# Up projections of four feed-forward blocks from seven products of quarters in place of eight, with the down projections in three groups

## The chip, the cores and the metric

The kernel runs on one NeuronCore of a Trainium2 chip. The metric is the time of one execution on the device in microseconds, taken as the median of several runs. TensorE (PE) multiplies, VectorE (DVE), ScalarE (ACT) and GpSimd (POOL) work elementwise, and SyncE (SP) issues nearly all transfers.

## The reference

Two layers of a hybrid model on 512 tokens of width 1024, all in float32. Each layer has a feed-forward block (FFN), a mixer (attention of several kinds) and a second FFN; a norm follows at the end. The change touches only the four FFNs.

```python
def swiglu_ffn(x, g, w_gate, w_up, w_down):      # w_gate, w_up: 1024 x 2816; w_down: 2816 x 1024
    h = rmsnorm(x, g)
    return (jax.nn.silu(h @ w_gate) * (h @ w_up)) @ w_down

for i in range(DEPTH):
    x = x + 0.5 * swiglu_ffn(x, ffn1_norm[i], ...)
    x = x + mixer(rmsnorm(x, mix_norm[i]), ...)   # even_mixer for i = 0, odd_mixer for i = 1
    x = x + 0.5 * swiglu_ffn(x, ffn2_norm[i], ...)
return rmsnorm(x, final_norm)
```

## The kernel before

The activations stand transposed: x is eight tiles of 128 features by 512 tokens. To keep float32 accuracy, every operand is split into a high part and the rest (low part), and each product is three matmuls (mm3, lines 309 to 312): high by high, high by low, low by high. A weight tile takes a transfer (raw), a cast on ACT for the high part (wh, L305) and a subtraction on DVE for the low part (wl, L306). The norm is folded in: x times its gain is split into xg, and the reciprocal root mean square of each token (rb, a row that is broadcast to all partitions and copied from PSUM by ACT, L546) is multiplied onto the results.

An FFN is a loop over eleven pairs of hidden tiles (256 of the 2816 columns each). For a pair, gate_up_pair makes the gate product into two PSUM tiles psS and the up product into two tiles psT: 96 matmuls of 512 columns. Behind them, for each half, stands a chain over three engines: DVE multiplies gate by rb (L603), ACT takes silu (L604), POOL multiplies by rb again (L605), DVE multiplies by up (L607), ACT casts the result (L484), and DVE subtracts for its low part (L485). After six pairs, and after the other five, the down projection runs over the hidden tiles made so far (proj_T, results transposed, 512 columns wide). In the last FFN the down is proj_N, whose results are in natural order and which uses matmuls of 256 columns.

The mixers' weights are split ahead of time during the FFNs (cut_ahead): a generator whose units are taken between pairs and between downs, each of which loads a weight tile into buffers of its own (craw, ch, cl), splits it and stores both parts to memory.

A program of instructions for each engine is built ahead of time by a scheduler, which chooses an order for each engine from the code and the dependencies. On the chip every engine then runs its instructions strictly in that order, each waiting for the semaphores of what it needs. A tile has a tag with a fixed number of buffers (W_BUFS = 3 for wh and for wl), and a tile that reuses a buffer waits for its last reader.

Of the kernel before, what the change touches and what calls it, by code (L numbers as in the profile page):

```python
# [64 lines left out]
def hybrid_kernel(tc, x_in, positions, ffn1_norm, ffn1_w_gate, ffn1_w_up, ffn1_w_down, mix_norm,  # L65
# [4 lines left out]
    with ExitStack() as ctx:  # L70
# [6 lines left out]
        def nm(p):  # L77
            cnt[0] += 1
            return f"{p}_{cnt[0]}"
# [469 lines left out]
        def update(c, ps, scale, nxt):  # L549
            if scale == 1.0:  # L550
                nc.vector.tensor_add(x[c], ps, x[c])  # L551
            else:
                nc.vector.scalar_tensor_tensor(x[c], ps, scale, x[c], op0=ALU.mult, op1=ALU.add)
            if nxt is not None:
                nxt.add(c)


        def gate_up_pair(wg, wu, f0, norm, first):
# [49 lines left out]
                ats.append(split(a))  # L608
            return ats

        def ffn(norm, wg, wu, wd, nxt, hook=None, ahead=iter(()), per=1):

            f0 = 0
            for npair in (6, 5):
                at = []
                for k in range(npair):
                    at += gate_up_pair(wg, wu, f0 + 256 * k, norm, f0 == 0 and k == 0)
                    if hook is not None and f0 == 0:
                        next(hook, None)
                    if f0 or k > 1:  # L620
                        run(take(ahead, per))
                for d0 in range(0, D, 256):
                    run(proj_T(wd[f0:f0 + 256 * npair], at, d0,
                               lambda c, ps: update(c, ps, 0.5, nxt if npair == 5 else None)))
                    if npair == 6 or d0 < 512:
                        run(take(ahead, per))
                f0 += 256 * npair

        def final_ffn(norm, wg, wu, wd):
            gf = [tile_("pt", F32), tile_("pt", F32)]  # L630
            for hf in range(2):
                nc.scalar.dma_start(gf[hf], final_norm[hf * 512:(hf + 1) * 512].unsqueeze(0).to_broadcast([P, 512]))
            xn = [[tile_("m", F32), tile_("m", F32)] for _ in range(NT)]
            f0 = 0
            ssq, part, rn = small(4 * NT), small(NT), small(NT)

            def natural(t):
# [38 lines left out]
                    nc.sync.dma_start(out[t * P:(t + 1) * P, 512:1024], xn[t][1])  # L676
                return f

            for npair in (6, 5):
                at = []  # L680
                for k in range(npair):
                    at += gate_up_pair(wg, wu, f0 + 256 * k, norm, f0 == 0 and k == 0)
                    if f0 == 0 and 1 <= k <= 4:
                        natural(k - 1)
# [3 lines left out]
                f0 += 256 * npair  # L688


        def quarter_tiles():
# [721 lines left out]
```

## Time and profile before

| | |
|---|---|
| median of 3 runs | 2021.73 us (2020.76 to 2022.83) |
| the profiled execution | 2025.57 us |
| its span, first to last instruction | 2023.8 us |
| PE busy | 1983.0 us, 98% of the span |
| DVE busy | 1049.1 us, 52% |
| ACT busy | 771.3 us, 38% |
| POOL busy | 343.7 us, 17% |
| mean granted TensorE clock | 0.995 of 2.4 GHz |

The stages follow each other: the first FFN takes about 43 to 395 us, the even mixer to 684, the second FFN about 694 to 1064, the third 1075 to 1415, the odd mixer 1424 to 1640, the last FFN 1645 to 2018. The share of an engine over the whole span says little where stages differ, so the rows below are taken by stage. Matmuls are pipelined: the profile's duration of one (.39 us for 512 columns) is longer than the distance between the starts of two, and it is the distance that counts. L numbers are lines of the kernel that is profiled; in the changed kernel the same statements stand one line lower up to line 608 (L604 there is L603 here) and further down behind the new functions.

### The profile page before, as it was taken

How to read it: one execution, taken by the hardware profiler on the slowest of the kernel's cores; microseconds unless marked ns; L12 is line 12 of the kernel's file. 1: busy time of each engine (PE TensorE's matmuls, PEld its weight loads, DVE VectorE, ACT ScalarE, POOL GpSimd, SP SyncE). 2: the span in 40 equal slices, each digit the busy share in tenths (PEclk: the TensorE clock that was granted, in tenths of full speed). 3: DMA queues.
4: the chain of work that ended last, by engine and by line, in shares of the span. 5: the costliest groups of instructions: out<-in, count | busy, mean ns of one | idle time of the engine just before them, and what ended most of it. 6: DMA issues, size and time to landing. Idle time of an engine off the chain costs nothing.

```text
span 2023.8 us, 27480 instructions
## 1 busy us (share of the span) xinstructions
PE 1983.0 (98%) x10555; PEld 1708.0 (84%) x10555; DVE 1049.1 (52%) x1871; ACT 771.3 (38%) x1358; POOL 343.7 (17%) x412
## 2 busy tenths in 40 slices
PE   8999999999899999999999999999999999999998
PEld 6888888998888788888888888888999888899888
DVE  6654556446697634334353432344798754332433
ACT  5443344225577423213242231232346744221323
POOL 3110011223234211001121100111222321100112
PEclk9999999999999999999999999999999999999999
DMA  8998998792201423323323232223522243322321
GB/s 275 330 292 290 361 356 310 251 319 80 84 32 53 150 81 96 101 94 95 99 89 115 91 107 94 85 87 95 207 85 105 94 133 88 102 85 93 98 85 48
DMA packets 223604, 290.18 MB, mean 143 GB/s; under 512 B 25880, under 2 KB 191472, under 8 KB 223472
## 3 DMA queue, kind: packets, MB, share of 16 engines
q1 hardware_dynamic: 216544, 282.01, 42.0%
q10 hardware_dynamic: 6736, 6.37, 1.0%
q8 instruction: 83, 1.36, 0.3%
q14 instruction: 49, 0.40, 0.1%
q0 software_dynamic: 192, 0.04, 0.0%
HBM read 230.11 MB, written 58.26 MB: 142 GB/s over the span
## 4 chain that ended last, share of the span: by engine, by line
PE 87%; DVE 6%; DMA 2%; ACT 2%; issue 2%; POOL 1%; SPq 0%; ACTq 0%; POOLq 0%; DVEq 0%
PE psB L310 11%; PE psB L312 11%; PE psB L311 11%; PE psS L310 8%; PE psS L311 8%; PE psS L312 8%; PE psT L310 8%; PE psT L311 8%; PE psT L312 8%; PE psC L782 2%; PE psT L772 1%; DVE f L1241 1%; PE psS L747 1%; PE psS L746 1%; DVE sm L1240 1%
## 5 line engine op out<-in xcount | busy, mean ns | idle before, releaser
L306 DVE TENSOR_TENSOR wl<-raw,wh 128x1024 fp32r<-128x1024 f32 (+1 forms) x276 | 338.2, 1246 | 100.2 <-ACT wh L305 96.0
L305 ACT ACTIVATE wh<-raw 128x1024 fp32r<-128x1024 f32 (+1 forms) x276 | 274.8, 1013 | 206.2 <-PE psB L311 110.4
L605 POOL TENSOR_TENSOR p<-p,p 128x512 f32<-128x512 f32 x88 | 117.7, 1337 | 1026.0 <-ACT p L604 1026.0
L310 PE MATMUL psS<-xg,wh 128*128 128x512 f32 x704 | 275.9, 393 | 2.9 <-DVE x L551 2.1
L312 PE MATMUL psS<-xg,wl 128*128 128x512 f32 x704 | 274.4, 391 | 2.4 <-DVE wl L306 2.4
L311 PE MATMUL psS<-xg,wh 128*128 128x512 f32 x704 | 274.8, 391 | 0.9 <-DVE xg L507 0.9
L310 PE MATMUL psT<-xg,wh 128*128 128x512 f32 x704 | 274.5, 390 | 0.0
L312 PE MATMUL psT<-xg,wl 128*128 128x512 f32 x704 | 274.3, 390 | 0.0
L311 PE MATMUL psT<-xg,wh 128*128 128x512 f32 x704 | 274.2, 390 | 0.0
L310 PE MATMUL psB<-f,wh 128*128 128x512 f32 x528 | 205.4, 389 | 0.0
L311 PE MATMUL psB<-f,wh 128*128 128x512 f32 x528 | 205.4, 389 | 0.0
L312 PE MATMUL psB<-f,wl 128*128 128x512 f32 x528 | 205.4, 389 | 0.0
L603 DVE TENSOR_TENSOR p<-psS,p 128x512 f32<-128x512 f32 x88 | 60.3, 685 | 279.4 <-PE psS L312 270.2
L604 ACT ACTIVATE p<-p 128x512 f32<-128x512 f32 x88 | 55.6, 632 | 360.5 <-DVE p L603 359.8
L312 PEld LDWEIGHTS psS<-xg,wl 128*128 128x128 f32 x704 | 132.3, 188 | 31.2 <-DVE wl L306 3.7
L310 PEld LDWEIGHTS psS<-xg,wh 128*128 128x128 f32 x704 | 132.4, 189 | 30.6 <-DVE x L551 2.6
L311 PEld LDWEIGHTS psS<-xg,wh 128*128 128x128 f32 x704 | 132.5, 188 | 28.7 <-DVE xg L507 2.1
L311 PEld LDWEIGHTS psT<-xg,wh 128*128 128x128 f32 x704 | 132.5, 188 | 27.7
L312 PEld LDWEIGHTS psT<-xg,wl 128*128 128x128 f32 x704 | 132.4, 188 | 27.6
L310 PEld LDWEIGHTS psT<-xg,wh 128*128 128x128 f32 x704 | 132.3, 188 | 27.6
L310 PE MATMUL psB<-wh,xg 128*128 128x256 f32 x512 | 149.0, 291 | 0.4 <-PE psB L312 0.4
L312 PE MATMUL psB<-wh,xg 128*128 128x256 f32 x512 | 146.9, 287 | 0.0
(259 smaller groups left out, 3596.1 us busy)
## 6 DMA issues: line engine op xcount, KB each, us to landing
raw<-in_ffn_w_gate_dram SPq DMA_DIRECT2D x80, 512.0 KB, 5.1
raw<-in_ffn_w_up_dram SPq DMA_DIRECT2D x80, 512.0 KB, 5.0
raw<-in_ffn_w_down_dram SPq DMA_DIRECT2D x136, 256.0 KB, 3.7
cuth<-ch SPq DMA_DIRECT2D x44, 512.0 KB, 5.8
cutl<-cl SPq DMA_DIRECT2D x44, 512.0 KB, 5.8
wl<-cutl SPq DMA_DIRECT2D x44, 512.0 KB, 3.7
wh<-cuth SPq DMA_DIRECT2D x44, 512.0 KB, 4.4
raw<-in_ffn_w_down_dram SPq DMA_DIRECT2D x20, 512.0 KB, 3.5
```

The source lines that it names most:

```text
L305: pin(nc.scalar.activation(h[:, :n], raw[:, :n], AF.Copy))
L306: pin(nc.vector.tensor_sub(l[:, :n], raw[:, :n], h[:, :n].bitcast(F32)))
L310: nc.tensor.matmul(ps, lh, rh, start=start, stop=False)
L311: nc.tensor.matmul(ps, lh, rl, start=False, stop=False)
L312: nc.tensor.matmul(ps, ll, rh, start=False, stop=stop)
L603: nc.vector.tensor_mul(g, psg[f], rb)
L604: nc.scalar.activation(g, g, AF.Silu)
L605: nc.gpsimd.tensor_mul(g, g, rb)
L746: nc.tensor.matmul(bank[i], q[:, tsl], kh[:, 0:w], start=True, stop=False)
L747: nc.tensor.matmul(bank[i], q[:, tsl], kl[:, 0:w], start=False, stop=True)
L772: nc.tensor.transpose(ps[:, o:o + P], pr[i][:, j * P:(j + 1) * P], ident)
L782: nc.tensor.matmul(job["accs"][0][:, j * P:512], v(j), hl[j][part], start=first, stop=last)
```

## The change

Pair 0 of each FFN stays as it is, and behind it the sums of x are made once (class Sums, L627 to L637 of the changed kernel): from four pairs of x tiles, tokens 0 to 255 and 256 to 511, the right-hand terms of Strassen's products. For pairs 1 to 10 the up product (a 256 x 1024 by 1024 x 512 product) comes from seven products of quarters (seven): four sums of weight quarters on DVE (L681 to L684), their high and low parts (L665 on ACT, L666 on DVE), seven times 12 matmuls of 256 columns, and the combination of the results out of PSUM by two copies on ACT (L698, L702) and seven DVE operations. The seven results share four PSUM tiles psS: products 1 and 2, 3 and 5, 6 and 7 in one each. The gate product is as before, now in psT, behind the seven in the code. The activations of these pairs are L735 to L741. The down projection runs in three groups of 4, 4 and 3 pairs; in the last FFN the first two of them use proj_T. W_BUFS and RAW_BUFS are 4, the tag p has 8 buffers, and the cuts of the mixers' weights use the weights' buffers and are taken at pairs 4, 5, 8 and 9 and between downs.

```diff
+GROUPS = ((0, 4), (4, 8), (8, 11))
-SB_BUFS = {'xg': 18, 'f': 36, 'm': 8, 'p': 9, 'pt': 9}
+SB_BUFS = {'xg': 18, 'f': 36, 'm': 8, 'p': 8, 'pt': 9}
-W_BUFS = 3
-RAW_BUFS = 3
+W_BUFS = 4
+RAW_BUFS = 4
...
-                _, h, l = load_cut(src, a, b, rows, ("craw", "ch", "cl"), 2, 2)
+                _, h, l = load_cut(src, a, b, rows, ("raw", "wh", "wl"), RAW_BUFS, W_BUFS)
...
+        class Sums:
...
+            def make(self):
+                a, b = slice(0, 256), slice(256, 512)
+                for c in range(4):
+                    y = [tile_("p", F32) for _ in range(2)]
+                    for i in range(2):
+                        nc.scalar.activation(y[i], x[c + 4 * i], AF.Copy,
+                                             scale=gcol(self.norm.which, self.norm.layer, c + 4 * i))
+                    t = sb.tile([P, 1024], F32, tag="s7", bufs=3, name=nm("t7"))
+                    u1, u2, u3, u4 = (t[:, i * 256:(i + 1) * 256] for i in range(4))
+                    nc.vector.tensor_sub(u1, y[0][:, a], y[0][:, b])
+                    nc.vector.scalar_tensor_tensor(u2, u1, -1.0, y[1][:, b], op0=ALU.mult, op1=ALU.subtract)
+                    nc.vector.tensor_sub(u3, y[1][:, b], y[0][:, b])
+                    nc.vector.scalar_tensor_tensor(u4, u2, -1.0, y[1][:, a], op0=ALU.mult, op1=ALU.subtract)
+                    h, l = (sb.tile([P, 1024], F32R, tag="t7" + k, bufs=4, name=nm("t7" + k)) for k in "hl")
+                    nc.scalar.activation(h, t, AF.Copy)
+                    nc.vector.tensor_sub(l, t, h.bitcast(F32))
...
+        def seven(w, f0, sums, z):
...
+            parts(quarter(h1, 0), quarter(l1, 0), a11)
...
+            parts(h2, l2, raw[1])
...
+            nc.vector.tensor_add(s1, a21, a22)
+            nc.vector.tensor_add(s2, s1, a11)
+            nc.vector.tensor_add(s4, s2, a12)
+            nc.vector.tensor_add(s3, a11, a21)
+            for t, ns in ((u, (3, 5)), (v, (6, 7))):
+                h, l = new("wh", F32R, W_BUFS), new("wl", F32R, W_BUFS)
+                parts(h, l, t)
...
+            bank = [ps_tile("S") for _ in range(4)]
+            q = {n: bank[i // 2][:, (i % 2) * 256:(i % 2) * 256 + 256] for i, n in enumerate((1, 2, 3, 5, 6, 7, 4))}
...
+            for n in (1, 2, 3, 5, 6, 7, 4):
+                for c in range(4):
+                    mm3(q[n], st[n][0][:, c], st[n][1][:, c], *sums.term[n][c], c == 0, c == 3)
+                if n == 1:
+                    nc.scalar.copy(k1, q[1])
+                elif n == 2:
+                    nc.vector.tensor_add(z[0][:, a], q[2], k1)
+                elif n == 3:
+                    nc.scalar.copy(k3, q[3])
+                elif n == 5:
+                    nc.vector.tensor_add(k3, q[5], k3)
+                elif n == 6:
+                    nc.vector.tensor_add(k6, q[6], k1)
+                    nc.vector.tensor_add(z[0][:, b], k6, k3)
+                elif n == 7:
+                    nc.vector.tensor_add(k6, q[7], k6)
+                    nc.vector.tensor_add(z[1][:, b], q[5], k6)
+                else:
+                    nc.vector.tensor_add(z[1][:, a], q[4], k6)
+
+        def gate_up(wg, wu, k, norm, sums):
+
+            if k == 0:
+                at = gate_up_pair(wg, wu, 0, norm, True)
+                run(sums.work)
+                return at
...
+            seven(wu, f0, sums, up)
+            psg = [ps_tile("T"), ps_tile("T")]
...
-            for npair in (6, 5):
+            sums = Sums(norm)
+            for p0, p1 in GROUPS:
...
-                    if f0 or k > 1:
+                    if k in (4, 5, 8, 9):
                         run(take(ahead, per))
...
-                for q in range(4):
-                    run(proj_N([cols_of(wd[f0:f0 + 256 * npair], 256 * q, 256)], at,
-                               fin_a(q) if npair == 6 else fin_b(q), last=npair == 5 and q == 3))
+                if p1 < 11:
+                    for d0 in range(0, D, 256):
+                        run(proj_T(wd[256 * p0:256 * p1], at, d0, lambda c, ps: update(c, ps, 0.5, None)))
+                    continue
```

Where the scheduler puts this is seen in the order of the engines' instructions. The first place is DVE behind pair 0 of the second FFN (the same stands there in each FFN). Before, these are the activations of pair 0 (L603, L607, L485) and of pair 1, with the low parts of the weights of pair 1 and 2 (L306) between them.

```order
L603 TENSOR_TENSOR p_6960<-psS_6809,p_6958 128x512 [waits Activation_49]
L607 TENSOR_TENSOR p_6964<-psT_6811,p_6960 128x512 [waits PE_49,Pool_49]
L603 TENSOR_TENSOR p_6970<-psS_6810,p_6958 128x512
L306 TENSOR_TENSOR wl_7076<-raw_7074,wh_7075 128x1024 [waits DMAHW7_49,DVE_49,Activation_49]
L485 TENSOR_TENSOR f_6967<-p_6964,f_6966 128x512 [waits Activation_49]
L607 TENSOR_TENSOR p_6974<-psT_6812,p_6970 128x512 [waits PE_49,Pool_49]
L485 TENSOR_TENSOR f_6977<-p_6974,f_6976 128x512 [waits Activation_49]
L306 TENSOR_TENSOR wl_7130<-raw_7128,wh_7129 128x1024 [waits DMAHW0_49,Activation_49]
```

Now the sums of x (t_1633, t_1638, t_1643, t_1648, 16 operations of 128x256) and their low parts (t7l, four of 128x1024) stand behind the same activations, and among them the sums of weight quarters (s_1659 and s_1660), of which L683 is the last.

```order
L604 TENSOR_TENSOR p_7678<-psS_7518,p_7666 128x512
L486 TENSOR_TENSOR f_7675<-p_7672,f_7674 128x512 [waits Activation_49]
L608 TENSOR_TENSOR p_7682<-psT_7520,p_7678 128x512 [waits PE_49,Pool_49]
L631 TENSOR_TENSOR t_1633_7692<-p_7688 128x256 [waits Activation_49]
...
L637 TENSOR_TENSOR t7l_7724<-t_1643_7718,t7h_7723 128x1024 [waits Activation_49]
L634 SCALAR_TENSOR_TENSOR t_1648_7731<-t_1648_7731,p_7728 128x256 [waits DVE_49]
L682 TENSOR_TENSOR s_1660_7755<-s_1659_7754,raw_7742 128x512 [waits DVE_49]
L684 TENSOR_TENSOR s_1660_7755<-raw_7742 128x512
L637 TENSOR_TENSOR t7l_7737<-t_1648_7731,t7h_7736 128x1024 [waits Activation_49]
L683 TENSOR_TENSOR s_1659_7754<-s_1660_7755,raw_7744 128x512 [waits DVE_49]
L700 TENSOR_TENSOR p_7740<-psS_7768,k_1669_7772 128x256 [waits PE_49]
L666 TENSOR_TENSOR wl_7761<-s_1659_7754,wh_7760 128x1024 [waits Activation_49]
```

On PE the third product of that pair (psS_7769) follows the second (psS_7768) at once; its weights wh_7760 are ACT's cast of s_1659, the tile that L683 completes, and wl_7761 the last row above.

```order
L313 MATMUL psS_7768<-xg_7510,wl_7751 128x256
L311 MATMUL psS_7769<-xg_7462,wh_7760 128x256 [waits PE_49,Activation_49]
L312 MATMUL psS_7769<-xg_7463,wh_7760 128x256
L311 MATMUL psS_7770<-t7h_7697,wh_7764 128x256 [waits DVE_49,Activation_49]
L312 MATMUL psS_7770<-t7l_7698,wh_7764 128x256
L313 MATMUL psS_7769<-xg_7462,wl_7761 128x256 [waits DVE_49]
```

The second place is ACT in the middle of the third FFN. Before, a pair has silu (L604) and cast (L484) of each half with weight casts (L305) between, and nothing that PE waits for but those weights.

```order
L604 ACTIVATE p_9788<-p_9788 128x512 [waits DVE_49]
L305 ACTIVATE wh_9853<-raw_9852 128x1024 [waits DMAHW3_49,PE_49,Activation_49]
L484 CAST f_9794<-p_9792 128x512 [waits DVE_49]
L604 ACTIVATE p_9798<-p_9798 128x512 [waits DVE_49]
L305 ACTIVATE wh_9883<-raw_9882 128x1024 [waits DMAHW4_49,PE_49,Activation_49]
L484 CAST f_9804<-p_9802 128x512 [waits DVE_49]
```

Now the copies of products 1 and 3 out of PSUM (L698, L702) stand behind silu and cast (L736, L485) of the pair before.

```order
L736 ACTIVATE p_11376<-p_11376 128x512 [waits DVE_49,Pool_49]
L665 ACTIVATE wh_11418<-s_2350_11409 128x1024 [waits PE_49,Activation_49]
L485 CAST f_11381<-p_11186 128x512 [waits DVE_49]
L736 ACTIVATE p_11385<-p_11385 128x512 [waits DVE_49,Pool_49]
L698 COPY k_2359_11426<-psS_11422 128x256 [waits PE_49]
L306 ACTIVATE wh_11525<-raw_11524 128x1024 [waits DMAHW2_49,Activation_49]
L485 CAST f_11390<-p_11187 128x512 [waits DVE_49]
L702 COPY k_2360_11427<-psS_11423 128x256 [waits PE_49]
```

On PE the second product of the same pair (into psS_11422, weights wh_11404) waits for ACT, whose copy L698 reads psS_11422; it stands behind seven matmuls of the third product.

```order
L311 MATMUL psS_11423<-xg_10667,wh_11414 128x256 [waits Activation_49]
...
L313 MATMUL psS_11423<-xg_10681,wl_11415 128x256
L311 MATMUL psS_11423<-xg_10734,wh_11414 128x256
L311 MATMUL psS_11422<-xg_10667,wh_11404 128x256 [waits Activation_49]
L312 MATMUL psS_11422<-xg_10668,wh_11404 128x256
```

## Rows read from the trace of the kernel before

**Rows 1.** Busy time by stage: window, PE, PEld, DVE, ACT, POOL, granted clock, DMA share, GB/s.

```profile
43.00:395.00 352.00, 352.00 (x1569) 293.42 (x1568) 196.37 (x233) 142.38 (x176) 47.79 (x36) 1.00 0.91 314
716.00:1064.00 348.00, 348.00 (x1538) 288.15 (x1538) 144.25 (x158) 102.89 (x130) 41.62 (x30) 1.00 0.31 95
1666.00:2000.00 334.00, 334.00 (x1924) 295.70 (x1923) 126.08 (x151) 94.35 (x130) 36.16 (x31) 1.00 0.28 86
```

**Rows 2.** Chain of waits of PE: waited for, us in total, times, longest us.

```profile
PE psX L704 <- POOL f L1017: 4.6, 1, 4.6
```

**Rows 3.** Timeline of PE in the first FFN: start us, duration us, line, operation.

```profile
100.09 0.39 PE L312 MATMUL psS<-xg,wl 128*128 128x512 f32 x1
...
102.36 0.39 PE L310 MATMUL psS<-xg,wh 128*128 128x512 f32 x1
```

**Rows 4.** Timeline of PE in the last FFN's first down, 25 matmuls apart.

```profile
1799.95 0.28 PE L310 MATMUL psB<-wh,f 128*128 128x256 f32 x1
...
1802.95 0.28 PE L311 MATMUL psB<-wl,f 128*128 128x256 f32 x1
```

**Rows 5.** Groups by line and shape: busy us, mean ns of one, idle before them.

```profile
L306 DVE TENSOR_TENSOR wl<-raw,wh 128x1024 fp32r<-128x1024 f32 x252 | 319.5, 1289 | 97.7 <-ACT wh L305 93.4 <-DMA cutl<-cl 4.2
L650 DVE SCALAR_TENSOR_TENSOR m<-psB,m 128x256 f32<-128x256 f32 x28 | 10.6, 419 | 73.1 <-PE psB L312 73.1
L305 ACT ACTIVATE wh<-raw 128x1024 fp32r<-128x1024 f32 x252 | 260.5, 1050 | 198.1 <-PE psB L311 110.4 <-PE psB L312 51.4 <-issue 15.6
L484 ACT CAST pt<-psT 128x256 fp32r<-128x256 f32 x40 | 14.7, 367 | 6.2 <-PE psT L772 6.2
L605 POOL TENSOR_TENSOR p<-p,p 128x512 f32<-128x512 f32 x88 | 117.7, 1337 | 1026.0 <-ACT p L604 1026.0
```

**Rows 6.** Timeline of DVE: three weight subtractions in a run.

```profile
876.48 3.49 DVE L306 TENSOR_TENSOR wl<-raw,wh 128x1024 fp32r<-128x1024 f32 x3
```

**Rows 7.** Timeline of all engines behind pair 0 of the second FFN.

```profile
717.44 0.60 PE L544 MATMUL psX<-keep,sm 128*128 128x128 f32 x4
717.79 0.48 PE L310 MATMUL psS<-xg,wh 128*128 128x512 f32 x1
...
718.13 0.59 ACT L546 COPY p<-psX 128x512 f32<-128x512 f32 x1 [11.49 <-PE psX L544]
...
718.74 1.28 ACT L604 ACT_TABLE_LOAD   x1
718.75 0.69 DVE L603 TENSOR_TENSOR p<-psS,p 128x512 f32<-128x512 f32 x1 [2.69 <-ACT p L546]
...
720.03 0.63 ACT L604 ACTIVATE p<-p 128x512 f32<-128x512 f32 x1
...
720.74 1.29 POOL L605 TENSOR_TENSOR p<-p,p 128x512 f32<-128x512 f32 x1 [3.79 <-ACT p L604]
...
722.06 0.69 DVE L607 TENSOR_TENSOR p<-psT,p 128x512 f32<-128x512 f32 x1 [2.62 <-POOL p L605]
...
722.67 0.68 DVE L603 TENSOR_TENSOR p<-psS,p 128x512 f32<-128x512 f32 x1
722.78 0.62 ACT L484 CAST f<-p 128x512 fp32r<-128x512 f32 x1 [1.17 <-DVE p L607]
...
723.27 1.21 DVE L306 TENSOR_TENSOR wl<-raw,wh 128x1024 fp32r<-128x1024 f32 x1
723.38 0.63 ACT L604 ACTIVATE p<-p 128x512 f32<-128x512 f32 x1
...
724.09 1.53 POOL L605 TENSOR_TENSOR p<-p,p 128x512 f32<-128x512 f32 x1 [2.07 <-ACT p L604]
...
724.40 1.78 DVE L485 TENSOR_TENSOR f<-p,f 128x512 fp32r<-128x512 f32 x1
```

**Rows 8.** Chain that ended last, at the start of the run: start us, us, what.

```profile
8.98 0.85 PE psS L310 x2
9.83 0.85 PE psS L311 x2
10.68 0.63 PE psS L312 x2
11.32 0.23 PE psT L310
```

More of the change, by code (lines that the diff above doesn't have):

```diff
@@ L609, in gate_up_pair, with __init__ @@
             return ats
+        class Sums:
+            def __init__(self, norm):
+                self.norm = norm
+                self.term = {n: [None] * 4 for n in (1, 2, 3, 4, 5, 6, 7)}
+                self.work = self.make()
+            def make(self):
[14 more added lines that the diff above has]
+                    nc.vector.tensor_sub(l, t, h.bitcast(F32))
+                    for i, n in enumerate((5, 6, 7, 4)):
+                        self.term[n][c] = h[:, i * 256:(i + 1) * 256], l[:, i * 256:(i + 1) * 256]
+                    for n, i, sl in ((1, 0, a), (2, 1, a), (3, 1, b)):
+                        self.term[n][c] = tuple(t[:, sl] for t in self.norm.xg[c + 4 * i])
+                    yield
@@ new lines, in gate_up @@
+        def gate_up(wg, wu, k, norm, sums):
[3 more added lines that the diff above has]
+                return at
+            f0 = 256 * k
+            up = [tile_("p", F32) for _ in range(2)]
+            seven(wu, f0, sums, up)
+            psg = [ps_tile("T"), ps_tile("T")]
+            for hf in range(2):
+                h, l = wunit(wg[hf * 512:(hf + 1) * 512, f0:f0 + 256].rearrange("(c p) f -> p c f", p=P), 4, 256)
+                for f in range(2):
+                    for c in range(4):
+                        xh, xl = norm.xg[hf * 4 + c]
+                        mm3(psg[f], h[:, c, f * P:(f + 1) * P], l[:, c, f * P:(f + 1) * P], xh, xl,
+                            hf == 0 and c == 0, hf == 1 and c == 3)
+            rb = norm.rstd_row()
+            ats = []
+            for f in range(2):
+                g = tile_("p", F32)
+                nc.vector.tensor_mul(g, psg[f], rb)
+                nc.scalar.activation(g, g, AF.Silu)
+                nc.gpsimd.tensor_mul(g, g, rb)
+                if f == 0:
+                    nc.vector.tensor_mul(up[f], up[f], g)
+                else:
+                    nc.vector.scalar_tensor_tensor(up[f], up[f], -1.0, g, op0=ALU.mult, op1=ALU.mult)
+                ats.append(split(up[f]))
+            return ats
@@ L611, in ffn @@
         def ffn(norm, wg, wu, wd, nxt, hook=None, ahead=iter(()), per=1):
-            f0 = 0
-            for npair in (6, 5):
+            sums = Sums(norm)
+            for p0, p1 in GROUPS:
                 at = []
-                for k in range(npair):
-                    at += gate_up_pair(wg, wu, f0 + 256 * k, norm, f0 == 0 and k == 0)
-                    if hook is not None and f0 == 0:
+                for k in range(p0, p1):
+                    at += gate_up(wg, wu, k, norm, sums)
+                    if hook is not None and k < 6:
@@ L626, in ffn @@
+                    if p1 < 11 or d0 < 512:
                         run(take(ahead, per))
-                f0 += 256 * npair
         def final_ffn(norm, wg, wu, wd):
@@ L677, in fin_b @@
                 return f
-            for npair in (6, 5):
+            sums = Sums(norm)
+            for p0, p1 in GROUPS:
                 at = []
[L681 to L684, printed above, removed]
+                for k in range(p0, p1):
+                    at += gate_up(wg, wu, k, norm, sums)
+                    if p1 == 11 and k < 10:
+                        natural(2 * (k - p0))
+                        natural(2 * (k - p0) + 1)
+                if p1 < 11:
+                    for d0 in range(0, D, 256):
+                        run(proj_T(wd[256 * p0:256 * p1], at, d0, lambda c, ps: update(c, ps, 0.5, None)))
+                    continue
                 for q in range(4):
-                    run(proj_N([cols_of(wd[f0:f0 + 256 * npair], 256 * q, 256)], at,
-                               fin_a(q) if npair == 6 else fin_b(q), last=npair == 5 and q == 3))
-                f0 += 256 * npair
+                    run(proj_N([cols_of(wd[256 * p0:256 * p1], 256 * q, 256)], at, fin_b(q), last=q == 3))
         def quarter_tiles():
```

33 lines of the change are left out of this document (29 added, 4 removed).

## The prediction

> **What bounds the kernel now.** I read first the busy time by stage: in the three feed-forward stretches PE is busy for the whole window, all at the full granted clock, while DVE works 38 to 56% of the time and the DMA engines are near their limit only in the first FFN (.91, against .31 and .28) [rows 1]. The chain of waits of PE says the same: the longest wait of the run is one of 4.6 us in a mixer [rows 2]. So an FFN costs what its matmuls cost, and a change that removes matmuls gains as long as nothing makes PE wait. I read what a matmul costs from starts: 512 columns leave every (102.36-100.09)/10 = .227 us [rows 3], 256 columns every (1802.95-1799.95)/25 = .120 us [rows 4], 6% more than half.
>
> **What the matmuls give.** Ten of the eleven pairs of each FFN change. The up product of such a pair was 48 matmuls of 512 columns (10.88 us) and is 84 of 256 (10.08): -.80 a pair, -32 over 40 pairs. The first two groups of the last FFN's down turn from 768 matmuls of 256 columns (92.2) to 384 of 512 (87.05): -5.1. Together **-37 us**. By the Trainium skill (page "TensorE: Matmul & The Clock Gate", section "Back-to-back issue gap") matmuls follow each other every N/2.4 + 2.5 ns; by that the same counts would give -48 (1536 fewer at .216, 2592 more at .109), an estimate from the page. The rows have both sizes slower, and the smaller one by more, so the rows decide.
>
> **The first Strassen pair of each FFN (k=1).** This is the largest term. The order of PE there is: product n=1 (12 matmuls), n=2 (12), then n=3, whose weights are the cast of a sum (s4) that DVE makes last (L683). All else PE could do, the gate product, stands behind. In front of L683 on DVE stand the activations of pair 0 and all the sums of x: 16 operations of 128x256 and 4 of 128x1024, because the sums are made once, right behind pair 0. Before, only pair 0's activations stood there, and PE had 96 matmuls with weights long ready.
>
> I put the new order onto the times of the same place before, T=0 being 717.79, where PE starts the pair behind the broadcast of the norm [rows 7]. The copy of the norm ends on ACT, the table load for silu takes until 2.24, silu of half 0 until 2.87; only then does ACT reach the copy of n=1's result that n=2 waits for, about .37 (a 256-column read from PSUM [rows 5]). n=2 starts at 3.26 in place of 12 x .120 = 1.44. Half 0 goes on: POOL 2.95 to 4.24, DVE's product 4.27; DVE's first product of half 1 at 4.88, silu 5.59, POOL 6.30 to 7.59, DVE's second product 7.62. Behind it DVE owes five more 512-wide operations (spacing .60 to .62, 722.06 to 722.67 to 723.27 [rows 7]), four of 1024 (3.49/3 = 1.16 in a run [rows 6]) and sixteen of 256 (.419 alone, about .36 in a run if the same .06 overlaps [rows 5]): 6 x .62 + 4 x 1.16 + 16 x .36 = 14.1. L683 ends at 21.7, ACT's cast (1.05 [rows 5]) at 22.9. PE had 24 x .120 = 2.9 of work: 20.0 us lost. The low part of the weights comes 1.2 later and PE has only 4 matmuls for that: .7. Then PE has stood still. What that costs in clock the start of the run shows, where PE also comes from a wait: its matmuls of 512 columns step at .85/2 = .43 (1.2 GHz) and then at .23 (2.4 GHz), and the 2.34 us from 8.98 to 11.32 hold six of them, 1.0 more than 6 x .227 [rows 8]. Sum 21.7, taken as **22 per FFN, +88**. Lower bound 18 (256-wide sums at a quarter of 1.16, no clock loss, low part hidden), upper 24 (chains of dependent sums that don't overlap, and casts on ACT between them): 72 to 96. The casts of the sums (ACT, 4 x 1.05 and 8 x .63) run beside and are shorter.
>
> **The other pairs.** The seven results lie two or three to a PSUM tile, so n=2 waits for ACT's copy of n=1, n=5 for ACT's copy of n=3, n=7 for DVE's sum with n=6; between each pair of these PE has other products to cover the wait: in 24 of 40 pairs 7 matmuls (.84), 4 (.48) and 1.9 us. Both copies stand in ACT's queue behind the last pair's activations. T=0 is now the first matmul of n=1. Gate half 0 was ready 12 matmuls (2.72) before. DVE's product -2.5, silu -1.75, POOL -1.04 to .25; DVE waits for POOL (.29), and only then takes half 1's product (.92); silu of half 1 1.69 to 2.32; copy of n=1 until 2.69. PE wanted it after 19 matmuls, 2.28: .4 lost. Now the cast of half 1 stands before the copy of n=3. Its POOL step could start at 2.4, but DVE is in a weight subtraction from 1.55 to 2.76. In [rows 7] such a step, started at 724.09, took 1.53 in place of 1.29 and ended 1.14 after the subtraction (724.48), and DVE's next one, started 724.40, ended only .56 after POOL (725.62). So POOL ends at 3.90, DVE's last product starts near 4.45, the cast ends 5.75, the copy 6.12; PE wanted it after 40 matmuls, 4.80 + .4: .9 lost. **1.3 to 1.4 a pair, 24 x 1.4 = +34.** Without the POOL collision it is .6 to .8 (+19), with half a weight cast ahead of the copy 1.9 (+46). n=7 has 1.9 us of cover and costs nothing as long as DVE is at most that late. The Trainium skill (page "SBUF — State Buffer", section "Who interferes with whom") says that a DVE instruction with two SBUF inputs and a GpSimd one that reads SBUF share a port, and that whoever is first blocks the other wholly. The rows just read agree; without such a lock this term would be the lower end.
>
> **Smaller terms.** The eight pairs that start a later group have a down in front, whose cover is longer: .4 each, and k=1 once more 1 each for its n=5: **+7** (3 to 12). The last group has three pairs in place of five: its down has four ready chunks of six, 24 x .227 = 5.4 us, in front of the last pair's activations, which need about 7 (half 0's product, then .71 + .71 + 1.33 + .72 + .6 + .7 of half 1 by the steps of [rows 7]): **+5** over four FFNs (0 to 8). The cuts now share the weights' buffers and come only at k=4, 5, 8, 9 and between downs. In the first FFN the DMA engines are at .91 already [rows 1]; a burst of cuts can make weights late there, or a fourth buffer can cover it: **+5** (0 to 20). DVE's own new work outside k=1 is four sums, seven combining operations and one and a half more weight subtractions a pair, 4 x .62 + 7 x .36 + 1.5 x 1.16 = 6.7 us. I cost it at nothing save where named: DVE is busy 144 of 348 us in the second FFN [rows 1], 41%, and 6.7 in a pair of some 21 us make that 73%. If that cover were gone, rival C is what it gives.
>
> **Sum.** -37 + 88 + 34 + 7 + 5 + 5 = +102 on a span of 2023.8. The profiled execution took 2025.6, 3.8 above the median of 2021.7; I add the sum to the median: **2124 us**, 5.0% slower. All lower ends give +57 (2079), all upper ones +145 (2167).
>
> **Rivals.**
> A, the forecast: 2124, its own range 2100 to 2150.
> B, only the k=1 wait: ACT reaches the copies in time and a pair loses just what a copy takes beyond its cover, .28 (start and end .1 each, copy .37, .2 of matmul end against .48): -37 + 88 + 11 = +62, 2084. For it: the steady ACT is only 28 to 40% busy. Against: the copies stand behind the casts in the written order.
> C, buffers: cuts in the shared buffers and the POOL collisions hold back weights too, each pair pays 1.9 and the first FFN 20: 2160. For it: .91 of DMA in the first FFN. Against: four raw buffers in place of three.
> D, the other side: the sums of x are hidden. If the k=1 wait is under 4 us each, and other pairs lose .4 at most, -37 + 16 + 5 = -16: 2006. It decides below (37 - 16)/4 = 5 us at k=1. Against it: 14 us of DVE work stand ahead of L683 in the order and PE has 3 us; DVE would have to run five times faster than its rows.
> E, the scheme saves nothing and costs nothing measurable: the DVE sums hidden as to half, the pairs' waits gone (k=1 at 9 us): -37 + 36, about 2021.
>
> **Chances.** A .70, B .13, C .10, D .05, E .02. What a measurement of this kernel tells from no change is about 0.2%, 4 us. A, B and C are all slower: .93; E .02 same; D .05 faster. The range 2079 to 2167 holds A, B and C; since each end stacks all bounds, I take 2080 to 2165.
>
> **What would show it.** Right: in each FFN one PE wait of about 20 us on n=3's weights, released by ACT's L665 behind DVE's L683, with DVE busy all through it; in the other pairs waits of .4 and .9 in front of n=2 and n=5, released by the copies L698 and L702; 256-column matmuls every .120. A step is wrong if the k=1 gap is under 15, if 256-column products of the sums step slower than .120, if waits on DMA appear in the middle stages, or if n=7 waits for DVE. The forecast falls if DVE runs the sums before pair 0's second half, or if PE stays at half clock long after each gap; then more than 1.0 is lost each time.

## The result, and the profile after

The changed kernel takes 2148.9 us (median of 4 runs, 2147.0 to 2150.8) against 2022.3 for the kernel before in the same runs: a ratio of 1.0622, 95% interval 1.0602 to 1.0642. That is 126.7 us more; 2124 had been forecast, in a range of 2080 to 2165.

The page of the profile after: its span, the busy time of each engine, and PE and its clock in 40 slices.

```profile
span 2146.7 us, 30520 instructions
...
PE 1991.9 (93%) x11611; PEld 1748.7 (81%) x11611; DVE 1403.5 (65%) x2495; ACT 910.5 (42%) x1566; POOL 349.4 (16%) x412
...
PE   6899999999999969999996999999999996999998
...
PEclk9899999989999989999998999999999998999999
```

PE is idle for 155 us in place of 41, and busy for 9 us more, though the forecast takes 37 us of matmul time out. A busy share is not a sum of steps here: a matmul of 256 columns is recorded as .28 us where the next one starts after .12, and as .41 at half clock. Some slices stand out with a 6, and their clock is below full: these are the places where PE stands still for long.

The chain of waits of PE says on what it stood (waited for, us in total, times, longest us). Of before, the longest wait was 4.6 us [rows 2].

```profile
PE psS L311 <- ACT wh L665: 71.2, 6, 17.7
PE psS L311 <- ACT k L698: 20.5, 28, 1.8
PE psS L311 <- ACT k L702: 15.9, 26, 0.7
...
PE psX L840 <- DVE sa L891: 3.0, 1, 3.0
...
PE psS L313 <- DVE wl L666: 2.8, 2, 1.7
PE psT L311 <- DMA wh<-cuth: 2.7, 1, 2.7
```

The first three lines are the three waits of the forecast: the cast of the weight sum at pair 1 (four long ones), and the copies of products 1 and 3. The one transfer among the lines shown, the last, is in the even mixer.

The timeline behind pair 0 of the second FFN answers to [rows 7]; T=0 is the matmul of 760.41.

```profile
760.05 0.60 PE L545 MATMUL psX<-keep,sm 128*128 128x128 f32 x4
760.41 0.36 PE L311 MATMUL psS<-xg,wh 128*128 128x256 f32 x1
...
763.59 0.39 PE L311 MATMUL psS<-xg,wh 128*128 128x256 f32 x1 [1.50 <-ACT k L698]
...
765.00 0.28 PE L313 MATMUL psS<-xg,wl 128*128 128x256 f32 x1
783.02 0.58 PE L311 MATMUL psS<-xg,wh 128*128 128x256 f32 x1 [17.73 <-ACT wh L665]
...
784.35 0.42 PE L312 MATMUL psS<-t7l,wh 128*128 128x256 f32 x1
784.56 0.42 PE L313 MATMUL psS<-xg,wl 128*128 128x256 f32 x1
...
788.40 0.33 PE L312 MATMUL psS<-t7l,wh 128*128 128x256 f32 x1
788.57 0.28 PE L313 MATMUL psS<-t7h,wl 128*128 128x256 f32 x1
788.69 0.28 PE L311 MATMUL psS<-t7h,wh 128*128 128x256 f32 x1
```

And the end of DVE's work ahead of it, with the cast on ACT that PE waits for:

```profile
768.06 0.69 DVE L608 TENSOR_TENSOR p<-psT,p 128x512 f32<-128x512 f32 x1 [1.33 <-POOL p L606]
768.67 0.41 DVE L631 TENSOR_TENSOR t<-p 128x256 f32<-128x256 f32 x1
...
780.04 1.23 DVE L637 TENSOR_TENSOR t7l<-t,t7h 128x1024 fp32r<-128x1024 f32 x1
781.19 0.69 DVE L683 TENSOR_TENSOR s<-s,raw 128x512 f32<-128x512 f32 x1
...
781.91 2.00 ACT L665 ACTIVATE wh<-s 128x1024 fp32r<-128x1024 f32 x2 [1.90 <-DVE s L683]
```

DVE is busy for 13.71 of the 13.82 us from 768.06 to 781.88, and L683 is its last step, at T=21.5 (forecast 21.7). PE starts n=3 at T=22.6 (forecast 22.9). From 783 to 788.4 it steps at .21 a matmul of 256 columns, half clock (1.2 GHz), and only then at .12.

Where the time went by stage, worked out from the starts of PE's matmuls in each trace: an FFN counts from the broadcast of its norm (L544 before, L545 after; this leaves pair 0 to the stage ahead, and ends the first FFN before the change at 380 us, where the mixer's matmuls begin, not at 395) to the last matmul of its last wide down, and the last FFN to the last matmul of the run.

| us | FFN 1 | even mixer | FFN 2 | FFN 3 | odd mixer | FFN 4 to end | median of the runs |
|---|---|---|---|---|---|---|---|
| before | 338.2 | 337.2 | 337.5 | 337.5 | 252.9 | 348.3 | 2022.3 |
| changed | 369.6 | 352.0 | 364.5 | 364.3 | 254.2 | 371.9 | 2148.9 |
| e1, pair 1 plain | 349.5 | 344.5 | 347.8 | 346.4 | 257.0 | 353.5 | 2069.7 |
| e2, tiles | 360.3 | 353.1 | 353.5 | 352.2 | 254.8 | 359.2 | 2104.6 |
| e3, gate first | 375.8 | 352.9 | 358.3 | 359.1 | 254.5 | 362.3 | 2129.1 |
| e4, cuts apart | 396.1 | 359.9 | 364.1 | 365.1 | 254.4 | 369.8 | 2182.9 |
| e5, three edits | 337.2 | 354.0 | 331.8 | 331.9 | 258.6 | 338.8 | 2023.3 |
| e6, three raw | 391.2 | 352.9 | 362.8 | 363.5 | 254.4 | 366.9 | 2161.5 |
| e7, down only | 338.2 | 342.9 | 337.5 | 337.5 | 253.2 | 343.2 | 2028.3 |
| e8, cuts from 2 | 370.6 | 338.9 | 361.4 | 360.7 | 254.2 | 369.7 | 2126.4 |
| e9, e5 + e8 | 352.2 | 338.8 | 336.1 | 337.6 | 256.8 | 339.9 | 2039.2 |
| e10, cuts from 4 | 345.2 | 338.0 | 332.4 | 332.9 | 258.5 | 339.4 | 2020.7 |
| e11, 16 places | 344.0 | 337.2 | 332.5 | 332.5 | 257.0 | 339.5 | 2016.2 |

The four FFNs take 108.7 us more; the even mixer, whose own code the change does not touch, takes 14.8 more. The stages are those of one profiled execution each, the median that of all; the profiled execution of e3 was the slowest of its four (2136.0 us).

### The profile page after: what moved, and what is told of

It reads as the page before. It is cut to its first block, busy times and chain, and to the rows that moved or that the text cites. A ratio compares the mean times of both kernels' runs of the same rounds, so it can differ in the third digit from the quotient of the medians.

```text
span 2146.7 us, 30520 instructions
## 1 busy us (share of the span) xinstructions
PE 1991.9 (93%) x11611; PEld 1748.7 (81%) x11611; DVE 1403.5 (65%) x2495; ACT 910.5 (42%) x1566; POOL 349.4 (16%) x412
## 5 line engine op out<-in xcount | busy, mean ns | idle before, releaser
L306 ACT ACTIVATE wh<-raw 128x1024 fp32r<-128x1024 f32 (+2 forms) x256 | 254.0, 996 | 333.5 <-PE psS L312 77.4
L307 DVE TENSOR_TENSOR wl<-raw,wh 128x1024 fp32r<-128x1024 f32 (+2 forms) x256 | 301.3, 1181 | 125.1 <-ACT wh L306 107.6
L311 PE MATMUL psS<-xg,wh 128*128 128x256 f32 (+1 forms) x544 | 169.1, 311 | 91.6 <-ACT wh L665 70.9
L311 PE MATMUL psS<-t7h,wh 128*128 128x256 f32 x640 | 189.4, 296 | 16.6 <-ACT k L702 15.9
L311 PEld LDWEIGHTS psS<-xg,wh 128*128 128x128 f32 x544 | 105.9, 195 | 103.4 <-ACT wh L665 71.7
L313 PE MATMUL psS<-t7h,wl 128*128 128x256 f32 x640 | 180.0, 285 | 2.8 <-DVE wl L666 2.8
L312 PE MATMUL psS<-t7l,wh 128*128 128x256 f32 x640 | 180.6, 285 | 0.0
L312 PE MATMUL psS<-xg,wh 128*128 128x256 f32 (+1 forms) x544 | 162.0, 300 | 0.0
L313 PE MATMUL psS<-xg,wl 128*128 128x256 f32 (+1 forms) x544 | 161.1, 301 | 0.4 <-DVE wl L307 0.2
L311 PE MATMUL psB<-wh,xg 128*128 128x256 f32 x512 | 149.5, 292 | 2.0 <-ACT f L1398 1.2
L665 ACT ACTIVATE wh<-s 128x1024 fp32r<-128x1024 f32 x80 | 84.1, 1059 | 157.4 <-PE psT L312 96.5
L311 PEld LDWEIGHTS psS<-t7h,wh 128*128 128x128 f32 x640 | 123.6, 193 | 32.1 <-ACT k L702 22.7
```

What stands on the lines that cost most here:

```text
L306: pin(nc.scalar.activation(h[:, :n], raw[:, :n], AF.Copy))
L307: pin(nc.vector.tensor_sub(l[:, :n], raw[:, :n], h[:, :n].bitcast(F32)))
L311: nc.tensor.matmul(ps, lh, rh, start=start, stop=False)
L312: nc.tensor.matmul(ps, lh, rl, start=False, stop=False)
L313: nc.tensor.matmul(ps, ll, rh, start=False, stop=stop)
L665: nc.scalar.activation(h, src, AF.Copy)
```

## The experiments

**e1, pair 1 as before the change.** The sums stay behind pair 0 in the code, and PE has a plain pair to work on.

```diff
                 run(sums.work)
                 return at
+            if k == 1:
+                return gate_up_pair(wg, wu, 256, norm, False)
```

> Pair 1 of each FFN is made as before the change (eight products), and the sums of x are built while PE works on it; Strassen starts at pair 2. Theory: the 22 us per FFN at pair 1 are lost only because the sums stand ahead of L683 while PE has 24 matmuls left. Then pair 1 costs .8 more, its wait is gone, and at pair 2 L683 still stands behind the POOL step of pair 1's second half, so n=3 starts near 10 us in place of 2.9, about 7.5 lost with clock. Net -16 per FFN, 2085 us (2070 to 2100). Rival: DVE as a whole is short of time, so its 14 us of sums are paid wherever they stand: the wait only moves to pair 2 or spreads over it, 2125 us or more.

2069.7 us, ratio to the kernel before 1.0231 (1.0216 to 1.0246). Its waits of PE from 760 to 1130 us (the rest of the second FFN from the middle of pair 2 on, and the start of the third), and the waits of the second FFN's first Strassen pair in the timeline:

```profile
PE psS L311 <- ACT k L702: 4.1, 6, 0.8
PE psS L311 <- ACT k L698: 2.9, 3, 2.1
PE psS L311 <- ACT wh L665: 2.7, 2, 2.6
```

```profile
757.97 0.39 PE L311 MATMUL psS<-xg,wh 128*128 128x256 f32 x1 [1.61 <-ACT k L698]
762.23 0.58 PE L311 MATMUL psS<-xg,wh 128*128 128x256 f32 x1 [2.58 <-ACT wh L665]
```

The wait on L665 of 17.7 us is 2.6 there, and all that pair 2 loses is 6.5 to 8.0 us an FFN (the starts of its matmuls beyond .227 and .120); 7.5 had been expected. The FFNs fell by 17 to 20 us each. The same 16 + 4 operations on DVE cost at most a third of what they did when PE has 22 us of its own work beside them: the rival, by which the whole price is paid wherever they stand, is out. It ended 15 us below the expectation: the FFNs gave 73 in place of 64, and the even mixer 7.5 (352.0 to 344.5), which nothing in the theory had.

**e2, other places in PSUM.** The seven results keep four tiles, but neighbours in time no longer share one. The tag S gets a fourth buffer with it, so the fourth tile of a pair no longer takes the place of its first; the two parts of the edit were not run apart.

```diff
-PSUM_BUFS = {'B': 4, 'S': 3, 'T': 4, 'C': 2, 'X': 2}
+PSUM_BUFS = {'B': 4, 'S': 4, 'T': 4, 'C': 2, 'X': 2}
...
-            q = {n: bank[i // 2][:, (i % 2) * 256:(i % 2) * 256 + 256] for i, n in enumerate((1, 2, 3, 5, 6, 7, 4))}
+            q = {n: bank[i % 4][:, (i // 4) * 256:(i // 4) * 256 + 256] for i, n in enumerate((1, 2, 3, 5, 6, 7, 4))}
```

> Only the places of the seven results in PSUM change: 1 and 6, 2 and 7, 3 and 4 share a tile, 5 has its own, in place of 1 and 2, 3 and 5, 6 and 7. Theory: n=2 and n=5 wait only since their tile is still to be read by a copy that stands behind activations in ACT's queue; with 48 and 36 matmuls between, the copies are done in time. 24 pairs lose 1.2 to 1.35 us less and the others some, -35 to -45: 2109 us (2100 to 2118); the pair-1 wait stays, since n=3 is set by L683. Rival: ACT and DVE are late by themselves, so that the waits come back at n=6, n=7 or at the weights: 2135 us or more.

2104.6 us, 1.0404 (1.0388 to 1.0419), 44 us less than the changed kernel. All waits of PE in the second FFN are three lines, against lines of 17.7 (L665), 4.4 (L702) and 4.0 (L698) there before this edit:

```profile
PE psS L311 <- ACT wh L665: 19.5, 1, 19.5
PE psT L311 <- DVE p L710: 0.9, 1, 0.9
PE psS L311 <- DVE p L700: 0.6, 1, 0.6
```

The waits on the copies L698 and L702 are gone, and but for 1.5 us on DVE's sums (L700, L710) nothing came in their place in this FFN; the one at pair 1 grew by 1.8 us, about what n=2 no longer waits there, since n=3 starts when L683 lets it.

**e3, the gate product first.** The call of seven moves behind the gate's matmuls.

```diff
-            up = [tile_("p", F32) for _ in range(2)]
-            seven(wu, f0, sums, up)
             psg = [ps_tile("T"), ps_tile("T")]
...
+            up = [tile_("p", F32) for _ in range(2)]
+            seven(wu, f0, sums, up)
             rb = norm.rstd_row()
```

> In each Strassen pair the gate product is made first and the seven behind it. Theory: PE then has 48 matmuls of 512 columns (10.9 us) ahead of n=1, so at pair 1 the wait on L683 falls from 22 to about 11, and in the other pairs the copies of n=1 and n=3 come when ACT has long finished the pair before, so n=2 and n=5 lose only some .3 together: -44 - 30 to -40, 2070 us (2055 to 2090). Rival: the copies' time is set by PSUM reads and not by the queue: only the pair-1 part, 2105 us; or the weights of the gate product, now needed first, come late: 2110 us and more, with waits on wh or wl in every pair.

2129.1 us, 1.0517 (1.0500 to 1.0535): 20 us less than the changed kernel, not 79. Its waits over the whole run:

```profile
PE psS L311 <- ACT wh L665: 31.0, 12, 6.0
PE psB L311 <- ACT f L485: 12.5, 10, 2.9
PE psS L311 <- ACT k L698: 10.6, 4, 2.8
PE psB L312 <- DVE f L486: 8.3, 11, 1.7
```

The pair-1 part came: the long wait fell from 17.7 to at most 6.0. Of the copies, L702 is gone and L698 halved. But up is now ready last, so the chain behind it (L739 or L741, the cast, the low part) stands bare in front of every down: 12.5 and 8.3 us of waits on L485 and L486, which in the changed kernel come to nothing and .2. The expectation had not counted what is queued behind a product that is moved to the end. What raised the first FFN above the changed kernel's (375.8) was not looked into.

**e4, cuts in buffers of their own.**

```diff
-                _, h, l = load_cut(src, a, b, rows, ("raw", "wh", "wl"), RAW_BUFS, W_BUFS)
+                _, h, l = load_cut(src, a, b, rows, ("craw", "ch", "cl"), 1, 2)
```

> The cuts of the mixers' weights have their own buffers again (one raw, two of each part), all else as in the changed kernel. The even mixer took 15 us more than before the change, with waits on transfers (2.7 and 2.6 us) and 17 us at half clock at its start. Theory: the shared buffers let cuts come late and crowd the transfers there; with own buffers 8 to 18 us come back, 2136 us (2130 to 2142). Rival: it is the prefetch of FFN weights into four buffers that crowds them: no change, 2149 us.

2182.9 us, 1.0790 (1.0773 to 1.0806): 34 us more, and both sides were wrong. The first FFN carries most of it (396.1). With one raw buffer for cuts, ACT stands in front of their casts until the transfer has landed (what ACT waits for, 120 to 400 us):

```profile
ACT ch L306 <- DMA craw<-in_ev_w_out_dram: 26.8, 8, 5.3
ACT ch L306 <- DMA craw<-in_ev_w_in_dram: 25.0, 8, 5.0
```

and behind them stand the copies that PE waits for: L698 costs it 10.9 us in four waits there. The edit leaves one raw buffer for the cuts where the kernel before had two, so it shows only that buffers of their own of this size are worse; it does not show that the shared ones are free. In the changed kernel's first FFN ACT waits 25.8 us and DVE 14.8 for stores of cuts to leave a shared buffer (120 to 400 us), of which PE feels little: 2.8 us of waits on low parts there.

The even mixer did not get better either (359.9), and this run tells against the theory. With buffers of their own the cuts run ahead of their places: the last load of a mixer weight to be cut is issued at 312 us, 124 us before the first FFN ends (396 in the changed kernel, 12 us before). The mixer is late all the same. PE waits there five times on loads of another weight of the mixer, and behind the first three of these waits the granted clock is .50 (1.2 GHz) from 467.4 to 484.5 us.

```profile
PE psC L1102 <- DMA pt<-in_ev_cmp_w_k_dram: 4.5, 5, 1.3
```

**e6, three raw buffers.**

```diff
-RAW_BUFS = 4
+RAW_BUFS = 3
```

> The changed kernel with three raw buffers in place of four. Theory: transfers of FFN weights that run ahead into the fourth buffer crowd the even mixer's start; with three its 352 us fall to 337 to 344, at 0 to 6 us more in the FFNs: 2140 us (2134 to 2149). Rival: the crowd is the reload of the mixer's own weights, which nothing here changes: the mixer stays at 350 to 354 us, 2149 us or more.

2161.5 us, 1.0682 (1.0665 to 1.0699). The mixer stays at 352.9, as the rival said; the first FFN pays 21.6 us. So the fourth buffer does not crowd the mixer and is needed in the first FFN.

**e7, the down projection alone.** The kernel before, with the loops over GROUPS and proj_T in the last FFN, nothing else.

```diff
-            for npair in (6, 5):
+            for p0, p1 in GROUPS:
...
-                    at += gate_up_pair(wg, wu, f0 + 256 * k, norm, f0 == 0 and k == 0)
+                    at += gate_up_pair(wg, wu, 256 * k, norm, k == 0)
```

> The kernel before with only the down projection changed: three groups of 4, 4 and 3 pairs, the last FFN's first two transposed. No Strassen, buffers and cuts as before. Theory: -5.1 from the matmuls of the last FFN, and up to +5 since the last group has only three pairs in front of its down: 2019 us (2015 to 2024). Rival: more and shorter groups leave DVE's and ACT's chains uncovered at each of the four added starts of a down: 2028 us or more.

2028.3 us, 1.0031 (1.0019 to 1.0043): slower by .3%, though the last FFN is 5.1 us shorter, as the matmul counts say. The other FFNs are unchanged to .1 us: with the plain pairs a group of three costs nothing at its down. What was lost is again in the even mixer, +5.7, and neither expectation had the place. No cut stands late here: the last load for one is issued at 211 us, 169 us before the FFN ends. What PE meets in the mixer is that of e4, waits on loads of in_ev_cmp_w_k and a stretch at half clock (the window's columns are those of [rows 1]); the kernel before has one such wait (1.2 us, on in_ev_cmp_w_v) and a full clock there. Why these loads come later was not traced.

```profile
PE psC L968 <- DMA pt<-in_ev_cmp_w_k_dram: 2.2, 4, 1.5
```

```profile
410.00:423.70 13.70, 13.16 (x60) 12.42 (x59) 1.58 (x8) 0.39 (x2) 0.73 (x4) 0.50 0.75 236
```

**e8, the cuts at other pairs.**

```diff
-                    if k in (4, 5, 8, 9):
+                    if k > 1:
```

> The changed kernel with the mixers' cuts taken at every pair from 2 on, as before the change, in place of pairs 4, 5, 8 and 9; shared buffers as in the change. Theory: the last four cuts of the first FFN fall behind its end and crowd the even mixer's start; spread, they are done earlier, the mixer falls to 338 to 345 us and the first FFN pays up to 5: 2140 us (2133 to 2148). Rival: cuts in shared buffers hold up the weights of the pair they stand in: the first FFN gains more than 10 us, 2155 us or more.

2126.4 us, 1.0509 (1.0494 to 1.0524): 22.6 us less than the changed kernel, and below the range of the expectation. The even mixer is back at 338.9, for 1 us more in the first FFN; the three later FFNs fell by 3.1, 3.6 and 2.2, which the theory did not have. Two units of a cut are taken at each place in the first FFN; the change has 14 places for 32 units, so four are left and come at its end, in front of the mixer's own loads. (The kernel before has 15 places, two units short as well, but its cuts had buffers of their own and ran ahead: the last load for one is issued at 214 us.) The first 42 us of the mixer in the changed kernel, and of e11 (below), which leaves none: window, PE, PEld, DVE, ACT, POOL, granted clock, DMA share, GB/s.

```profile
408.00:450.00 42.00, 36.28 (x204) 34.42 (x204) 14.59 (x58) 5.38 (x12) 4.52 (x4) 0.89 0.94 308
```

```profile
383.00:425.00 42.00, 41.67 (x289) 40.36 (x289) 16.11 (x65) 6.51 (x16) 6.37 (x10) 1.00 0.80 262
```

With the transfers at .94 PE got 204 matmuls through in place of 289. It waits 2.7 us at 411 for the first reloaded weight (wh<-cuth) and 2.6 at 440.57 for a load of in_ev_cmp_w_k, and the granted clock is .50 (1.2 GHz) from 440.3 to 457.4 us. In e11 neither wait and no such stretch is there.

**e5, three edits.** e1 and e2 together, and the gate product ahead of the seven at pair 2 alone.

```diff
-            seven(wu, f0, sums, up)
+            if k != 2:
+                seven(wu, f0, sums, up)
...
+            if k == 2:
+                seven(wu, f0, sums, up)
             rb = norm.rstd_row()
```

> The edits of e1 and e2 together, and in pair 2 alone, the first with seven products, the gate product made ahead of the seven. Theory: the three waits are separate places and add up: 2069.7 of e1, less 42 for the tiles (e2's -44 without its small part at pair 1), less 26 for pair 2, where n=3 comes 10.9 us later and L683 is done: 2002 us (1995 to 2012), below the 2023 of the kernel before. Rival: with PE faster, DVE (65% busy in the changed kernel) becomes the bound and waits on wl or on combinations spread over the pairs: 2020 to 2035 us.

2023.3 us, .9999 (.9989 to 1.0008): the same as before the change, not 1% below. In the second FFN no wait of PE is left, and it takes 331.8 us where its matmuls alone, at .227 and .120, take 330.4. So the three edits together take the waits out, and the rival (DVE as the new bound) does not show, with DVE busy 68% of the span. The 21 us that are missing from the forecast have two halves. Against e1, from which it was counted, the FFNs fell by 57.5 us and not by 68: PE's starts come 70 us late there in e1 and still 13 in e5, half of that in the first FFN. The mixers rose by 11, to 354.0 and 258.6, which is 16.8 and 5.7 over before. What the odd mixer's 4 to 6 us in e5 to e11 are was not traced.

**e9 to e11, e5 with the cuts elsewhere.** From pair 2 on (e9), from pair 4 on (e10), and at 16 places, which are just 32 units (e11):

```diff
-                    if k in (4, 5, 8, 9):
+                    if k in (4, 5, 6, 8, 9, 10):
```

> e5 with the edit of e8: the cuts taken at every pair from 2 on. In e5 the four FFNs are 1 to 6 us shorter than before the change, as expected, but the even mixer behind the first FFN takes 354 us in place of 337 and the odd one 259 in place of 253. Theory: that loss is set by where the cuts stand and is independent of the FFN edits, so the 13 us of e8 in the even mixer come back here: 2008 us (2003 to 2014), .5 to 1% faster than before. Rival: faster FFNs leave the transfers less time, so that the mixer stays at 350 us or the first FFN waits longer: 2018 us or more, the same as before.

> e5 with the cuts taken at every pair from 4 on (e5: pairs 4, 5, 8, 9; e9: from 2 on). In e9 the even mixer fell to 339 us as expected, but the first FFN rose from 337 to 352 and the others by 1 to 6, with waits on wl around pairs 2 and 3. Theory: those waits come of cuts standing between the sums and the first Strassen pair, where DVE has no room; from pair 4 on all 32 units still fit into the first FFN, so the mixer stays near 340 and the first FFN falls to 338 to 343: 2010 us (2004 to 2016). Rival: in the first FFN any earlier cut is paid by the same amount, since DVE and the transfers have no room anywhere: 2023 us or more.

> e5 with the cuts taken at pairs 4, 5, 6, 8, 9 and 10: just the 32 units of the even mixer in the first FFN, none at pair 7. Theory as for e10: once no cut is left behind the end of the first FFN the even mixer is at 338 to 342 us, 2010 us (2004 to 2016); if instead the mixer stays at 350, the loss there is not of the cuts left over, and the time is that of e5, 2023 us.

e9: 2039.2 us, 1.0083 (1.0068 to 1.0097). The mixer fell to 338.8 as it should, but the first FFN rose to 352.2 and the two after it by 4 to 6. The gain that was expected was not to be had that way: the rival's second half was right, and PE waits in the first FFN for low parts and sums:

```profile
PE psS L313 <- DVE wl L666: 4.4, 4, 2.2
PE psS L311 <- ACT wh L665: 2.1, 2, 1.4
```

e10: 2020.7 us, .9983 (.9974 to .9993), 11 over its expectation and outside its range. e11: 2016.2 us, **.9964 (.9950 to .9978)**, 6 over and at its range's edge. The mixer is at 338.0 and 337.2, as expected, the first FFN at 345.2 and 344.0, above the 338 to 343 of the theory. Away from the first Strassen pairs the cuts cost 7 to 8 us in the first FFN and give back 16 to 17 in the mixer. e11 beats both kernels, by .4% and by 6.2%. The change that cost 127 us is worth 7.5 when its three waits are taken out and the cuts have their places. The wider matmuls of the last down are in this with about 5 us (e7), and seven products are then made in nine pairs of eleven.

## Why the prediction was right, and where it was too low

**The matmuls (-37).** The counts at .227 and .120 (1488 matmuls of 512 columns before, 1008 of 512 and 840 of 256 after) give 337.8 us before and 329.6 after for each of the first three FFNs, -8.2 each; e7 shows the -5.1 of the last down by itself. Matmuls of 256 columns stepped at .120 in the products of the sums as well. The estimate of -48 beside this term is -49 by its own counts; nothing hangs on it.

**Pair 1 (+88).** Added up from the starts of PE beyond .227 and .120 in the first 32 us of each FFN: 22.0, 22.6, 21.5 and 23.0, together 89.1. The step was right to its parts: n=2 at 3.18 (3.26 forecast), L683's end at 21.5 (21.7), n=3 at 22.6 (22.9). One part was mis-sized: the clock. The 19 matmuls from 784.35 to 788.40 took 4.05 us where 19 x .120 are 2.28: 1.8 us and not 1.0; the forecast took its price from the start of the run, where fewer were at half clock. With the first steps behind 783.02, which also wait for the second cast of L665, PE lost 2.7 us there. The low part of the weights, for which .7 had been set, was not waited for (the matmul of 784.56 follows the one of 784.35 at half-clock distance). e1 shows the cause: the wait falls from 17.7 to 2.6 when the sums have other work of PE beside them.

**The other pairs (+34, +7, +5 and +5).** The starts that come more than .05 us late in the rest of the four FFNs add up to 57.5, against 51. One of the 13 pairs that lose 1.3 to 1.4, in the third FFN (T=0 at 1301.15):

```profile
1302.66 1.22 DVE L666 TENSOR_TENSOR wl<-s,wh 128x1024 fp32r<-128x1024 f32 x1
1302.84 0.63 ACT L736 ACTIVATE p<-p 128x512 f32<-128x512 f32 x1
1303.37 0.35 ACT L698 COPY k<-psS 128x256 f32<-128x256 f32 x1
1303.55 1.48 POOL L737 TENSOR_TENSOR p<-p,p 128x512 f32<-128x512 f32 x1 [2.13 <-ACT p L736]
...
1303.78 0.38 PE L311 MATMUL psS<-xg,wh 128*128 128x256 f32 x1 [0.20 <-ACT k L698]
1303.79 1.79 DVE L486 TENSOR_TENSOR f<-p,f 128x512 fp32r<-128x512 f32 x1
1305.50 0.68 DVE L741 SCALAR_TENSOR_TENSOR p<-p,p 128x512 f32<-128x512 f32 x1
...
1306.21 0.62 ACT L485 CAST f<-p 128x512 fp32r<-128x512 f32 x1 [1.52 <-DVE p L741]
1306.74 0.36 ACT L702 COPY k<-psS 128x256 f32<-128x256 f32 x1
...
1307.15 0.39 PE L311 MATMUL psS<-t7h,wh 128*128 128x256 f32 x1 [0.60 <-ACT k L702]
```

n=2 starts at 2.63 (forecast 2.7), n=5 at 6.0 (6.1); by the starts they are .36 and .76 late, and the matmul behind each restart another .1: 1.3, as set. e2 takes 44 us out, nearly all here. So rival B, waits of .28 a pair, is out. POOL's step began under a DVE subtraction, took 1.48 and ended 1.15 after it, and L486 behind it took 1.79: the collision of [rows 7] again. The rule of the Trainium skill (page "SBUF — State Buffer", section "Who interferes with whom"), that one of the two blocks the other wholly, agrees. No run takes the collision away by itself, so its share of the .76 is argued, not shown.

Pair by pair the sum is less close than its total. The 24 pairs that the forecast priced at 1.4 lost 43.3 (1.8 on average): ten of them lose 1.8 to 3.1. In eight of the ten a sum of weight quarters stands on DVE among the activations of the pair before, as L682 here in the second FFN, where n=2 is .9 late in place of .36; in a ninth, in the first FFN, DVE waits 1.7 us for the store of a cut.

```profile
937.08 0.69 DVE L739 TENSOR_TENSOR p<-p,p 128x512 f32<-128x512 f32 x1 [1.18 <-POOL p L737]
937.69 0.68 DVE L682 TENSOR_TENSOR s<-s,raw 128x512 f32<-128x512 f32 x1
938.29 0.68 DVE L735 TENSOR_TENSOR p<-psT,p 128x512 f32<-128x512 f32 x1
```

These sums are part of the new work of DVE that the forecast costed at nothing. Four pairs that are neither among the 24 nor start a group (two each in the first and the last FFN) had no term and lost 6.7. The eight that start a group lost 5.4, of +7, and everything else 2.1, of +5 and +5: for the last downs PE waits .2 in all. Terms that were too high covered part of those that were too low.

**What failed is the term for the cuts (+5).** It was looked for in the first FFN alone, as late weights there, and summed with nothing for the stages between the FFNs. The even mixer paid 14.8 us. In the changed kernel the cause is units of the cuts left over at the end of the FFN, in front of the mixer's loads: the four runs without them (e8 to e11) have the mixer at 337 to 339, those with them at 344.5 to 354. The prediction counted the places of the cuts and did not count their units against them. But left-over units are not the only way to this loss: e4 and e7 have none and pay 22.7 and 5.7 there, with the same waits on in_ev_cmp_w_k and the same half clock. What makes those loads late in them stays open.

Added up, the FFNs have -38 from matmuls and 89.1 and 57.5 from waits, together the 108.7 of the table; with 14.8 of the even mixer and -.6 of the other stages this is the difference of the two spans (2146.7 - 2023.8 = 122.9), against +102. The medians of the runs lie 3.8 us further apart than the spans.

**Rivals.** The result lies just inside A's own range (2100 to 2150), and C's time (2160) was nearer than A's 2124. C had the price of a pair nearly right (1.8 on average against its 1.9), but its first FFN of 20 did not come: the rest of the first FFN lost 17.9, the other three 12 to 14. PE's waits on transfers are in the mixer and at the run's start. D and E are out for the kernel as changed; e5 is E's time and e11 goes about half the way to D's, once the places are mended.

## What to carry to other kernels

Where a new operand is made by another engine, count what stands in front of its last step in that engine's order against the work PE has left at that point; the price is the whole difference (about 20 of the 22 us here), and a pair of plain work in between took two thirds of the loss away. Put results that are read out early into PSUM tiles whose next writer comes late. And after changing a loop, count the side work that was hung on its iterations: with buffers shared with the loop's own work it keeps to its places, and units that no longer fit are paid in the next stage, where nobody looks for them.

## What the runs showed of the hardware

After 17.7 us without work PE stepped at .213 a matmul of 256 columns (1.2 GHz) until 788.4 us; that wait cost at least 1.8 us more than its own time. In the even mixer of the changed kernel the granted clock was .50 from 440.3 to 457.4 us, with a wait of PE of 2.6 us that ended at 440.57; in the 15.3 us ahead it was 1.00. A DVE subtraction of 128x512 took .68 us alone and 1.79 beside POOL's product, which took 1.48 in place of 1.29.
